# One encoder layer on one core: the early block's products in plain fp32 with its norm factor at the evacuations, late norms between the gates, and the ends of rows in pieces

## The chip, the cores and the metric

The kernel runs on one core of a Trainium2 chip. The core has a matrix engine (TensorE; PE in the rows, PEld for its weight loads), VectorE (DVE), ScalarE (ACT), GpSimd (POOL) and SyncE (SP), each with its own instruction stream, and 16 DMA engines that carry what the streams' queues ask for. The metric is the device time of one execution in microseconds; lower is better.

## The reference

One encoder layer over 512 tokens of 2048 channels, all in fp32:

```
h = rmsnorm(x, attn_norm)
q | k | v | z | gate = h @ w_in          # 1024 | 1024 | 1024 | 2048 | 4096 columns
A = diff_attention(q, k, v)              # 8 heads, two softmaxes each, block-causal
B = spatial_gating(gelu(z))              # u * (W_s @ rmsnorm(v) + b), chunks of 128 tokens
x = x + (sig(g_A) * (A @ P_A) + sig(g_B) * (B @ P_B)) @ w_out
x = x + peer(rmsnorm(x, ffn_norm))       # 8 heads, 16 of 16384 experts per token and head
y = rmsnorm(x, final_norm)
```

In `peer`, q = h @ w_q is scored against two sets of 128 sub-keys; the 16 best pairs give 16 experts per head and token, with a softmax over their scores as gates. Expert e adds gelu(h · u_e) * gate * v_e. The inputs are as the reference draws them, some of them scaled.

## The kernel before, in words

The first 128 tokens (the early block, names with E or 0) go through everything up to their experts first; the other 384 (the late block, L) follow. Weights come as tiles of 512 KB, `raw`, on SP's DMA queue. Each tile is split into two parts of the format fp32r: ACT casts it to `wh`, VectorE subtracts that from `raw` and gets `wl`, and each product is three matmuls: high weights by high operand, high by low, low by high (`project_rows` L174 for the early block, with the operand `hE` as two parts; `mm3` for the late one). `wh` and `wl` have three buffers, `raw` four and, in the early part, three more.

The order of the early block is: load x, norm it (Square with sum on ACT, rsqrt on VectorE with one POOL step, scale by the factor and by `gain`, a broadcast of attn_norm), transpose and split into `hE` (L494 to L503); queries, keys, values (`qk`, `ve`); two products `vv` with the attention heads between them and two `uu` (L559 to L568); then eight pairs of a `gate` and a `branch` product (L590 to L600). At the start of that stage the three late norms stand (L584 to L588): each loads 128 tokens `xt` on ACT's queue, norms them and fills a part of `hh`, which the late block multiplies by. Then `wo`, the second norm, four `wq` products with the top-k searches, and `route`, which lists experts and gates.

The late block: attention, `merge` (16 gate/branch pairs for each of two branches), output product, `wq`. Of the late tokens' experts 96 sets of single rows are taken for some tokens, and the others are done densely: all experts' u (products `pa`, 256 steps of 24 matmuls) and all experts' v (products `pvt`, 256 steps). During the u steps two generators hand out pieces of other work: `rgen` (the late tokens' routing; a step earns a credit and pieces cost some) and `ggen` (gates as dense columns, `gs`, written to `g_d`). The product of u, after Gelu, is written to `ga_d`; the v stage reads `ga_d` (`vga`) and `g_d` (`vg`, 1152 KB, one for each group of 16 steps).

The experts that are taken row by row ("sets") are fetched by POOL's indirect DMAs into `gat` tiles; each set costs VectorE one 128x2048 product (L267 with u, L274 with v). `sparse_step` is called once per weight load and takes as many sets as `due` says, which interpolates between `knots` (L247): pairs of a load's number and how many sets are done by then. 240 loads lie before the u steps (`AT_U`).

In the v stage the ends of rows stand at fixed steps. At step 26 the early block's experts (`acc0`, which is `h2n`) get x1 added and are normed and written (`finish_rows` L1025). When the last set of a group has been added, `fold_rows` (L1031) sums the partitions of `accx` by four matmuls with a 0/1 matrix, ACT copies them back, and `finish_rows` follows at once. `weights` casts and splits two steps ahead of the products.

## Time and profile before

| | |
|---|---|
| median of 3 runs | 3428.65 us (3427.03 to 3431.07) |
| the profiled execution | 3429.19 us, span 3427.5 us |
| TensorE matmul busy | 3250.8 us, 95% |
| VectorE busy | 2879.8 us, 84% |
| ScalarE, GpSimd busy | 1624.9 us (47%), 646.9 us (19%) |
| mean granted clock of TensorE | 0.977 |
| moved by DMA | 1099.54 MB, 321 GB/s over the span |

The span is the time between the first and last instruction seen by the profiler; the execution's own time is 1.7 us longer. Stages, by the output tiles of TensorE: x0 and its norm to 23.4 us; q, k, v to 100.9; vv and uu with the heads to 166.4; gate and branch to 336.3; wo to 385; wq and top-k 390.2 to 460.3; late attention to 719; merges to 1278; output product to 1410; late wq 1425 to 1582; u steps to 2535; v steps to 3411. A stretch is read by its rows of busy time: where TensorE's falls short of the stretch's length or its granted clock (1.00 is 2.4 GHz, 0.50 is 1.2 GHz) is below 1.00, it has lost time. The time in square brackets at the end of a row is how long the engine stood idle before it, and what ended that.

### The profile page before, as it was taken

The page shows a single profiled execution, that of the slowest core. Times are in us where ns is not written, and L with a number is a line of the kernel's source. Part 1 is how long each engine was busy: PE and PEld are TensorE (multiplying, and loading weights), DVE is VectorE, ACT ScalarE, POOL GpSimd, SP SyncE. Part 2 cuts the span into 40 slices and gives each one's busy share as a digit, 9 for nine tenths or more (in the row PEclk, how much of TensorE's full clock was granted, in tenths as well). Part 3 has the DMA queues.
Part 4 walks back from the last instruction along what each step waited for, and adds up shares of the span by engine and source line. Part 5 has one row for each costly group of instructions (what it writes and reads, how often), then busy time and mean ns, then how long its engine had stood idle before and what let it go on. Part 6 is the DMA issues. An engine that isn't in the chain of part 4 may idle for free. (4 is left out here: it accounts for less than half of the span.)

```text
span 3427.5 us, 53633 instructions
## 1 busy us (share of the span) xinstructions
PE 3250.8 (95%) x20673; PEld 3056.0 (89%) x20673; DVE 2879.8 (84%) x3851; ACT 1624.9 (47%) x2431; POOL 646.9 (19%) x507
## 2 busy tenths in 40 slices
PE   7979899989999999899899999999899999989997
PEld 5757678879989998799889999999898999989997
DVE  7878887888888889899899998777768899979974
ACT  6767634332233233333453788887343333333333
POOL 0000000222232223323223322222221111111100
PEclk9999999999999999899999999999999999999998
DMA  8779843869999999898899999999999999989953
GB/s 314 270 287 354 316 154 99 302 234 360 367 354 344 363 364 415 308 333 317 307 338 348 321 360 378 371 373 378 375 326 336 340 361 360 347 295 364 359 208 129
DMA packets 280784, 1099.54 MB, mean 321 GB/s; under 512 B 28144, under 2 KB 81392, under 8 KB 217744
## 3 DMA queue, kind: packets, MB, share of 16 engines
q1 hardware_dynamic: 189664, 560.14, 45.0%
q0 software_dynamic: 66656, 481.47, 37.1%
q10 hardware_dynamic: 24208, 54.50, 4.3%
q8 instruction: 163, 2.67, 0.3%
q14 instruction: 93, 0.76, 0.1%
HBM read 1048.98 MB, written 46.92 MB: 320 GB/s over the span
## 5 line engine op out<-in xcount | busy, mean ns | idle before, releaser
L109 DVE TENSOR_TENSOR wl<-raw,wh 128x1024 fp32r<-128x1024 f32 x992 | 1204.7, 1221 | 381.7 <-ACT wh L804 244.6
L804 ACT CAST wh<-raw 128x1024 fp32r<-128x1024 f32 x512 | 536.6, 1050 | 809.6 <-PE pvt L1051 329.1
L145 ACT CAST wh<-raw 128x1024 fp32r<-128x1024 f32 x480 | 502.0, 1050 | 686.7 <-PE gate L159 187.9
L160 PE MATMUL pa<-h2H,wl 128*128 128x288 f32 x2048 | 615.5, 301 | 27.0 <-DVE wl L109 26.7
L158 PE MATMUL pa<-h2H,wh 128*128 128x288 f32 x2048 | 616.5, 301 | 15.6 <-ACT wh L804 15.6
L1050 PE MATMUL pvt<-aH,wh 128*128 128x288 f32 x2048 | 612.9, 299 | 12.1 <-ACT wh L804 12.1
L1052 PE MATMUL pvt<-aH,wl 128*128 128x288 f32 x2048 | 607.5, 297 | 6.2 <-DVE wl L109 6.2
L159 PE MATMUL pa<-h2L,wh 128*128 128x288 f32 x2048 | 609.4, 298 | 0.0
L1051 PE MATMUL pvt<-aL,wh 128*128 128x288 f32 x2048 | 606.3, 296 | 0.0
L160 PEld LDWEIGHTS pa<-h2H,wl 128*128 128x128 f32 x2048 | 389.1, 190 | 37.1 <-DVE wl L109 35.5
L158 PEld LDWEIGHTS pa<-h2H,wh 128*128 128x128 f32 x2048 | 389.5, 190 | 16.8 <-ACT wh L804 16.8
L1050 PEld LDWEIGHTS pvt<-aH,wh 128*128 128x128 f32 x2048 | 389.3, 190 | 14.2 <-ACT wh L804 13.5
L1052 PEld LDWEIGHTS pvt<-aH,wl 128*128 128x128 f32 x2048 | 390.2, 191 | 8.7 <-DVE wl L109 8.6
L1051 PEld LDWEIGHTS pvt<-aL,wh 128*128 128x128 f32 x2048 | 390.7, 191 | 0.5 <-issue 0.5
L159 PEld LDWEIGHTS pa<-h2L,wh 128*128 128x128 f32 x2048 | 389.5, 190 | 0.0
L274 DVE SCALAR_TENSOR_TENSOR h2n<-gat,slot_a,h2n 128x2048 f32<-128x2048 f32 x127 | 297.7, 2344 | 5.2 <-DMA gat<-in_v_emb,slot_e 5.2
L288 POOL DMA_INDIRECT gat<-in_v_emb,slot_e x128 | 204.4, 1597 | 484.1 <-DVE wl L109 266.0
L267 DVE SCALAR_TENSOR_TENSOR gat<-gat,h2n 128x2048 f32<-128x2048 f32 x128 | 293.2, 2291 | 0.0
L288 POOL DMA_INDIRECT gat<-in_u_emb,slot_e x128 | 151.9, 1187 | 446.8 <-DVE gat L267 315.5
L288 POOL DMA_INDIRECT gat<-in_u_emb,xslot_e x96 | 146.4, 1525 | 437.1 <-DVE wl L109 423.6
L274 DVE SCALAR_TENSOR_TENSOR accx<-gat,xslot_a,accx 128x2048 f32<-128x2048 f32 x96 | 224.9, 2342 | 1.3 <-DMA gat<-in_v_emb,xslot_e 1.2
L267 DVE SCALAR_TENSOR_TENSOR gat<-gat,score 128x2048 f32<-128x2048 f32 x96 | 219.3, 2284 | 4.7 <-DMA gat<-in_u_emb,xslot_e 4.7
(423 smaller groups left out, 5889.6 us busy)
## 6 DMA issues: line engine op xcount, KB each, us to landing
raw<-in_uT SPq DMA_DIRECT2D x256, 512.0 KB, 8.0
raw<-in_v_tiles SPq DMA_DIRECT2D x256, 512.0 KB, 6.8
raw<-in_e_nat SPq DMA_DIRECT2D x144, 512.0 KB, 5.1
raw<-in_w_nat SPq DMA_DIRECT2D x128, 512.0 KB, 5.9
raw<-in_w_in SPq DMA_DIRECT2D x112, 512.0 KB, 6.9
ga_d<-ga ACTq DMA_DIRECT2D x128, 144.0 KB, 6.7
g_d<-gs ACTq DMA_DIRECT2D x18, 1024.0 KB, 10.1
vg<-g_d SPq DMA_DIRECT2D x16, 1152.0 KB, 13.8
```

The lines of the kernel that those rows point to most:

```text
L109: return nc.vector.tensor_tensor(low, full, high.bitcast(F32), op=OP.subtract)
L145: nc.scalar.copy(hi, raw)
L158: mm(ps, hi[:, k, :], xh[:, k0 + k, c0:c1], start=first and k == 0, stop=False)
L159: mm(ps, hi[:, k, :], xl[:, k0 + k, c0:c1], start=False, stop=False)
L160: got = mm(ps, lo[:, k, :], xh[:, k0 + k, c0:c1], start=False, stop=last and k == 7)
L267: used = nc.vector.scalar_tensor_tensor(row, row, 1.0, h2n if g < 0 else h2x[g], op0=OP.mult, op1=OP.mult, accum_out=a)
L274: used = nc.vector.scalar_tensor_tensor(acc, row, a, acc, op0=OP.mult, op1=OP.add)
L288: got = nc.gpsimd.indirect_dma_start(out=row, out_offset=None, in_=items[i][0], in_offset=bass.IndirectOffsetOnAxis(ap=column(i, slot_e, x ...
L804: nc.scalar.copy(hi, src)
L1050: mm(pv, hi[:, j, :], aH, start=j == 0, stop=False)
L1051: mm(pv, hi[:, j, :], aL, start=False, stop=False)
L1052: mm(pv, lo[:, j, :], aH, start=False, stop=j == VG - 1)
```

## The change

- The start: x comes in four pieces of 512 columns on SP's and ACT's queues. Each piece is transposed as it is, scaled by attn_norm as a column (`gcol`, 128x16, on POOL's queue) into `hP` and split into `hE`. The norm factor `r0` is worked out beside that and multiplied in where the products are evacuated (the `scale` of mul, Gelu and Sigmoid). The 1 MB broadcast is gone.
- `vv`, `uu` (two each) and the four `wq` products take `raw` and the plain fp32 operand (`hP`, `h2P`): one matmul instruction per k-tile, no `wh`, no `wl`.
- The late norms stand behind the gate/branch pairs (0,0), (0,3) and (1,2); `gainL` and `xt` are loaded on POOL's queue.
- `knots`: sets begin at load 14 instead of 24, and 212 instead of 204 are done at the first u step.
- `merge` computes a gate one pair ahead of its branch.
- `vg` is loaded on ACT's queue instead of SP's.
- `rgen` has three more pauses of cost 1.8, around the Exp of the softmax and ahead of the transposes, and a step earns 1.8 instead of 1.7.
- The ends of rows are generators, moved on by one piece a step.

```diff
-    def load_split_ap(src, shape):
+    def load_raw(src, shape):
...
         nc.sync.dma_start(raw, src)
+        return raw
+
+    def load_split_ap(src, shape):
+        raw = load_raw(src, shape)
...
     def row_product(src, xx, name):
         ps = pp_tile(name)
-        project_rows(src, xx, [ps])
+        if isinstance(xx, tuple):
+            project_rows(src, xx, [ps])
+            return ps
+        nk = 2 * src.shape[0]
+        for kk in range(nk // 2):
+            w = load_raw(src[kk], [P, 2, 512])
+            for j in range(2):
+                k = 2 * kk + j
+                mm(ps, xx[:, k, :], w[:, j, :], start=k == 0, stop=k == nk - 1)
         return ps
...
-    knots = [(24, 0), (AT_U, 204), (AT_V - 8, U_END), (AT_V, U_END), (AT_V + 222, len(items))]
+    knots = [(14, 0), (AT_U, 212), (AT_V - 8, U_END), (AT_V, U_END), (AT_V + 222, len(items))]
...
+        yield 1.8
         nc.scalar.activation(gate, gate, AF.Exp)
+        yield 1.8
...
-    nc.sync.dma_start(x0, x[0:P, :])
+    for q, eng in enumerate((nc.sync, nc.scalar, nc.sync, nc.scalar)):
+        eng.dma_start(x0[:, 512 * q:512 * q + 512], x[0:P, 512 * q:512 * q + 512])
...
+    hP = h2n.rearrange("p (k t) -> p k t", k=KT)
+    for q in range(KT // 4):
+        ks = slice(4 * q, 4 * q + 4)
+        pt = transpose4(x0[:, 512 * q:512 * q + 512])
+        nc.vector.tensor_tensor(hP[:, ks, :], pt, gcol[:, ks].unsqueeze(2).to_broadcast([P, 4, P]), op=OP.mult)
+        split_pair(hE, (slice(None), ks, slice(None)), hP[:, ks, :])
     with tc.tile_pool(name="e1", bufs=1) as e1:
-        gain = e1.tile([P, D], F32, name="gain")
-        nc.scalar.dma_start(gain, bcast_rows(attn_norm, D))
-        hn = e1.tile([P, D], F32, name="hn")
-        norm_columns(hn, x0, row_scale(hn, x0), gain, 0, hE)
+        sqx = e1.tile([P, D], BF16, name="sqx")
+        r0 = ea.tile([P, 1], F32, name="r0")
+        nc.vector.tensor_copy(r0, row_scale(sqx, x0))
...
-            nc.scalar.copy(nat, row_product(src, hE, "qk"))
+            nc.scalar.mul(nat, row_product(src, hE, "qk"), r0)
...
-            nc.scalar.activation(vv[:, cs], row_product(w_nat[Z_NAT + c], hE, "vv"), AF.Gelu)
+            nc.scalar.activation(vv[:, cs], row_product(w_nat[Z_NAT + c], hP, "vv"), AF.Gelu, scale=r0)
...
-        nc.scalar.dma_start(gainL, bcast_rows(attn_norm, D))
-        for b in range(LB):
-            xt = em.tile([P, D], F32, name="xt")
-            nc.scalar.dma_start(xt, x[(b + 1) * P:(b + 2) * P, :])
+        nc.gpsimd.dma_start(gainL, bcast_rows(attn_norm, D))
+        xts = []
+
+        def fetch(b):
+            xts.append(em.tile([P, D], F32, name="xt"))
+            nc.gpsimd.dma_start(xts[b], x[(b + 1) * P:(b + 2) * P, :])
+
+        def norm_late(b):
             hn = em.tile([P, D], F32, name="hnL")
-            norm_columns(hn, xt, row_scale(hn, xt), gainL, b, hh)
+            norm_columns(hn, xts[b], row_scale(hn, xts[b]), gainL, b, hh)
+            if b + 1 < LB:
+                fetch(b + 1)
+
+        fetch(0)
...
+                if (br, c) in ((0, 0), (0, 3), (1, 2)):
+                    norm_late((3 * br + c) // 2)
...
-        h2E = operand(e2p, KT, P, "h2E", ("eH", "eL"))
-        norm_columns(h2n, x0, rsqrt(ss, 1, 1.0 / D, "xr"), gain, 0, h2E)
+        h2P = e2p.tile([P, KT, P], F32, tag="eH", name="h2P")
+        r = rsqrt(ss, 1, 1.0 / D, "xr")
+        for q in range(KT // 4):
+            qs = slice(q * 512, (q + 1) * 512)
+            nc.vector.scalar_tensor_tensor(h2n[:, qs], x0[:, qs], r, gain[:, qs], op0=OP.mult, op1=OP.mult)
+            nc.scalar.copy(h2P[:, 4 * q:4 * q + 4, :], transpose4(h2n[:, qs]))
...
-            nc.scalar.copy(nat, row_product(e_nat[EW + c], h2E, "wq"))
+            nc.scalar.copy(nat, row_product(e_nat[EW + c], h2P, "wq"))
...
+            ahead = [unit(0)]
             for n in range(KT):
-                pg = project(w_in[G0 + KT * br + n], hh, "gate")
-                sg = gt.tile([P, LN], F32, name="sg")
-                nc.scalar.activation(sg, pg, AF.Sigmoid)
+                if n + 1 < KT:
+                    ahead.append(unit(n + 1))
+                sg = ahead[n]
...
-            nc.sync.dma_start(
+            nc.scalar.dma_start(
                 gms[grp], g_d[:, :, grp * VG:(grp + 1) * VG, :].rearrange("c p e t -> p c e t"))
...
-                credit += 0.0 if i < 2 else 1.7
+                credit += 0.0 if i < 2 else 1.8
...
-        def finish_rows(acc, t0, n):
+        def finish_rows(acc, t0, n, before):
+            for _ in before():
+                yield
             scr = gat.tile([P, D], F32, tag="gat", name="gat")
...
+            nc.scalar.activation(scr, acc, AF.Square, accum_out=ss)
+            yield
...
+            nc.gpsimd.tensor_tensor(y, v, mhalf, op=OP.pow)
+            yield
...
+            nc.vector.scalar_tensor_tensor(scr, acc, y, fgain, op0=OP.mult, op1=OP.mult)
+            yield
+            yield
             nc.scalar.dma_start(out[t0:t0 + n, :], scr[:n, :])
...
         def fold_rows(accx, fold):
+            yield
             for q in range(4):
...
                 nc.scalar.copy(accx[:, cs], ps)
+                if q % 2:
+                    yield
...
+                ends.append(finish_rows(acc0, 0, P, add_first))
+            ends[:] = [e for e in ends if next(e, "end") != "end"]
             sparse_step(AT_V + step, folded)
```

Three places show how instructions moved. The first is ACT's stream at the start of the gate stage, behind the last two evacuations of uu (`utE`); `hnL` is the Square of a late norm, `hH` the evacuated transposes of one, `sgE` a gate's Sigmoid. Before:

```order
L583 DMA gainL<-in_attn_norm 128x2048
L586 DMA xt<-in_x 128x2048
L145 CAST wh<-raw 128x1024 x2
L212 ACTIVATE hnL,ss<-xt 128x2048
L145 CAST wh<-raw 128x1024 x2
L203 CAST hH<-pt 128x4x128
L145 CAST wh<-raw 128x1024
L203 CAST hH<-pt 128x4x128 x2
L586 DMA xt<-in_x 128x2048
L203 CAST hH<-pt 128x4x128
```

The same place now:

```order
L151 CAST wh<-raw 128x1024 x6
L226 ACTIVATE hnL,ss<-xt 128x2048
L624 ACT_TABLE_LOAD
L624 ACTIVATE sgE<-gate,r_185 128x512
L151 CAST wh<-raw 128x1024 x2
L217 CAST hH<-pt 128x4x128 x2
L151 CAST wh<-raw 128x1024 x3
L217 CAST hH<-pt 128x4x128 x2
L226 ACTIVATE hnL,ss<-xt 128x2048
```

The loads have left ACT's stream, six casts stand between uu and the first Square, and the second Square follows the first norm's last evacuation directly.

The second place is the first load of `vg`, late in the u steps. Before, on SP, among the weight tiles:

```order
L794 DMA raw<-in_uT 128x1024 x221
L911 DMA vg<-g_d 128x18x128
L794 DMA raw<-in_uT 128x1024 x2
L906 DMA vga<-ga_d 128x576
L794 DMA raw<-in_uT 128x1024 x2
```

Now, on ACT, where `g_d<-gs` is the write of the last gates and `ga` a Gelu of u products:

```order
L847 CAST wh<-raw 128x1024
L909 DMA g_d<-gs 128x2048
L847 CAST wh<-raw 128x1024
L938 ACTIVATE ga<-pa 128x288
L939 DMA ga_d<-ga 128x288
L954 DMA vg<-g_d 128x18x128
L847 CAST wh<-raw 128x1024 x2
```

The load stands two weight casts behind the write of the gates that it reads, and ahead of the next casts.

The third is ACT's stream at the first fold in the v stage; `accx<-yps` copies the folded rows back, `gat,ss<-accx` is their Square. Before:

```order
L804 CAST wh<-raw 128x1024 x3
L1036 COPY accx_24162<-yps 128x512 x4
L212 ACTIVATE gat,ss<-accx_24162 128x2048
L1029 DMA out_y<-gat 64x2048
L804 CAST wh<-raw 128x1024
```

Now:

```order
L847 CAST wh<-raw 128x1024
L1104 COPY accx_23650<-yps 128x512 x2
L847 CAST wh<-raw 128x1024
L1104 COPY accx_23650<-yps 128x512 x2
L847 CAST wh<-raw 128x1024
L1073 ACTIVATE gat,ss<-accx_23650 128x2048
L847 CAST wh<-raw 128x1024
L969 CAST aH<-vga 128x288 x2
L847 CAST wh<-raw 128x1024 x3
L954 DMA vg<-g_d 128x18x128
L1088 DMA out_y<-gat 64x2048
```

A cast of weights now stands between each two pieces, and the write of the rows is four casts behind the Square.

## Rows read from the trace of the kernel before

**Rows 1.** The page: busy time by engine, DMA share by slice, one group.

```profile
PE 3250.8 (95%) x20673; PEld 3056.0 (89%) x20673; DVE 2879.8 (84%) x3851; ACT 1624.9 (47%) x2431; POOL 646.9 (19%) x507
...
DMA  8779843869999999898899999999999999989953
...
L109 DVE TENSOR_TENSOR wl<-raw,wh 128x1024 fp32r<-128x1024 f32 x992 | 1204.7, 1221 | 381.7 <-ACT wh L804 244.6
```

**Rows 2.** Stretches: length, busy PE, PEld, DVE, ACT, POOL, PEclk, DMA share, GB/s.

```profile
100.90:166.40 65.50, 59.22 (x251) 44.26 (x251) 55.42 (x95) 47.83 (x74) 3.48 (x3) 0.92 0.75 250
166.40:336.30 169.90, 150.09 (x646) 115.81 (x645) 140.49 (x151) 119.54 (x128) 1.65 (x3) 0.96 0.88 321
230.90:336.30 105.40, 104.09 (x446) 81.57 (x445) 93.04 (x84) 79.42 (x81) 0.00 (x0) 1.00 0.98 356
390.20:460.30 70.10, 60.13 (x245) 47.60 (x246) 62.27 (x198) 37.51 (x41) 0.00 (x0) 0.86 0.62 216
1690.00:2090.00 400.00, 377.54 (x2755) 369.93 (x2754) 382.61 (x677) 262.59 (x473) 112.49 (x68) 0.98 0.93 342
2090.00:2400.00 310.00, 310.00 (x2377) 310.00 (x2377) 238.38 (x226) 254.47 (x474) 70.81 (x51) 1.00 0.98 376
2400.00:2535.00 135.00, 125.01 (x905) 122.92 (x904) 98.12 (x98) 48.07 (x66) 29.08 (x21) 0.97 0.96 364
2535.00:2690.00 155.00, 143.08 (x1036) 140.82 (x1035) 115.90 (x136) 60.26 (x87) 26.57 (x20) 0.96 0.91 324
...
3036.00:3066.00 30.00, 21.40 (x103) 16.69 (x102) 17.99 (x25) 9.68 (x13) 2.92 (x4) 0.83 0.48 148
3290.00:3312.00 22.00, 17.27 (x83) 13.54 (x83) 11.53 (x17) 8.09 (x11) 0.56 (x1) 0.82 0.29 88
```

**Rows 3.** Timeline of the start: start, us, engine, line, instruction, idle before.

```profile
11.75 1.91 ACT L212 ACTIVATE hn<-x 128x2048 f32<-128x2048 f32 x1 [9.21 <-DMA x<-in_x]
...
23.40 0.80 PE L183 MATMUL qk<-wh,hEH 128*128 128x512 f32 x1
```

**Rows 4.** Timeline: first passes of two k-tiles of a split product, full clock.

```profile
28.23 0.39 PE L183 MATMUL qk<-wh,hEH 128*128 128x512 f32 x1
...
28.93 0.40 PE L183 MATMUL qk<-wh,hEH 128*128 128x512 f32 x1
```

**Rows 5.** Timeline: weight loads of a plain fp32 product (second fold), full clock.

```profile
3297.30 0.19 PEld L1035 LDWEIGHTS yps<-accx,fold 128*128 128x128 f32 x1 [0.36 <-issue]
3297.73 0.19 PEld L1035 LDWEIGHTS yps<-accx,fold 128*128 128x128 f32 x1 [0.24 <-issue]
```

**Rows 6.** Timeline of wq: the first of three such waits.

```profile
416.65 0.79 PE L184 MATMUL wq<-wl,h2EH 128*128 128x512 f32 x1 [3.31 <-DVE wl L109]
```

**Rows 7.** Timeline of the gate stage: transposes of the first late norm.

```profile
188.04 1.09 PE L196 MATMUL pt<-ident,hnL 128*128 128x128 f32 x4 [11.07 <-DVE hnL L222]
```

**Rows 8.** Timeline at the end of the late attention.

```profile
753.72 0.87 PE L196 MATMUL pt<-ident,o 128*128 128x128 f32 x3 [5.79 <-DVE o L481]
```

**Rows 9.** Groups of 1581.8 to 2535; waits of 1655 to 2090 (total, times, longest).

```profile
L274 DVE SCALAR_TENSOR_TENSOR h2n<-gat,slot_a,h2n 128x2048 f32<-128x2048 f32 x56 | 131.3, 2345 | 3.5 <-DMA gat<-in_v_emb,slot_e 3.5
...
PEld pa L160 <- DVE wl L109: 31.5, 34, 3.0
```

**Rows 10.** DMA issues (KB, median us to landing), vg's of 2385 to 2415; timeline.

```profile
raw<-in_uT SPq DMA_DIRECT2D x256, 512.0 KB, 8.0
...
g_d<-gs ACTq DMA_DIRECT2D x18, 1024.0 KB, 10.1
...
vg<-g_d SPq DMA_DIRECT2D x1, 1152.0 KB, 20.7
...
2414.11 0.61 PE L158 MATMUL pa<-h2H,wh 128*128 128x288 f32 x1 [5.82 <-ACT wh L804]
```

**Rows 11.** Timeline of the v stage: behind acc0's end, and the first fold.

```profile
2639.22 0.61 PE L1050 MATMUL pvt<-aH,wh 128*128 128x288 f32 x1 [6.28 <-ACT wh L804]
...
3045.22 6.74 PE L1035 MATMUL yps<-accx,fold 128*128 128x512 f32 x8 [5.44 <-DVE accx L274]
```

More of the change, by code (lines that the diff above doesn't have):

```diff
@@ L69, in hybrid_block @@
     nc.gpsimd.dma_start(subln, diff_subln)
+    gcol = const.tile([P, KT], F32, name="gcol")
+    nc.gpsimd.dma_start(gcol, attn_col)
     gmn = const.tile([P, GROUPS], F32, name="gmn")
@@ L418, in route @@
                     nc.scalar.dma_start(xslot_g[g][to, :], gf[of])
+        yield 1.8
         pt = pt_tile("prt")
@@ L1023, in final_gain, with add_first @@
                 nc.vector.tensor_mul(ys[b][:c1 - c0, cs], ys[b][:c1 - c0, cs], fgain[:c1 - c0, cs])
-        def finish_rows(acc, t0, n):
+        def finish_rows(acc, t0, n, before):
+            for _ in before():
+                yield
             scr = gat.tile([P, D], F32, tag="gat", name="gat")
-            r = row_scale(scr, acc)
-            nc.vector.scalar_tensor_tensor(scr, acc, r, fgain, op0=OP.mult, op1=OP.mult)
-            nc.scalar.dma_start(out[t0:t0 + n, :], scr[:n, :])
+            ss = small.tile([P, 1], F32, name="ss")
+            nc.scalar.activation(scr, acc, AF.Square, accum_out=ss)
+            yield
+            v = small.tile([P, 1], F32, name="nrv")
+            y = small.tile([P, 1], F32, name="nry")
+            t = small.tile([P, 1], F32, name="nrt")
+            nc.vector.tensor_scalar(v, ss, 1.0 / D, EPS, op0=OP.mult, op1=OP.add)
+            nc.gpsimd.tensor_tensor(y, v, mhalf, op=OP.pow)
+            yield
+            nc.vector.tensor_mul(t, y, y)
+            nc.vector.tensor_mul(t, t, v)
+            nc.vector.tensor_scalar(t, t, -0.5, 1.5, op0=OP.mult, op1=OP.add)
+            nc.vector.tensor_mul(y, y, t)
+            nc.vector.scalar_tensor_tensor(scr, acc, y, fgain, op0=OP.mult, op1=OP.mult)
+            yield
+            yield
+            nc.scalar.dma_start(out[t0:t0 + n, :], scr[:n, :])
+        def add_first():
+            first = gat.tile([P, D], F32, tag="gat", name="gat")
+            nc.scalar.dma_start(first, x1_d[:P, :])
+            for _ in range(5):
+                yield
+            nc.vector.tensor_add(acc0, acc0, first)
+            yield
         def fold_rows(accx, fold):
+            yield
             for q in range(4):
@@ L1036, in fold_rows @@
                 nc.scalar.copy(accx[:, cs], ps)
+                if q % 2:
+                    yield
+        ends = []
         def folded(g):
-            fold_rows(accx[g], folds[g])
-            finish_rows(accx[g], *XG[g])
+            ends.append(finish_rows(accx[g], *XG[g], lambda: fold_rows(accx[g], folds[g])))
         for step in range(KT * NG):
@@ L1073, in hybrid_block @@
             if step == 20:
-                first = gat.tile([P, D], F32, tag="gat", name="gat")
-                nc.scalar.dma_start(first, x1_d[:P, :])
-            if step == 26:
-                nc.vector.tensor_add(acc0, acc0, first)
-                finish_rows(acc0, 0, P)
+                ends.append(finish_rows(acc0, 0, P, add_first))
+            ends[:] = [e for e in ends if next(e, "end") != "end"]
             sparse_step(AT_V + step, folded)
@@ L1083, in hybrid_block @@
                     nc.scalar.dma_start(ys[b][:c1 - c0, :], x1_d[T0 + c0:T0 + c1, :])
-        assert eaten[0] == len(items), (eaten, len(items))
+        assert eaten[0] == len(items) and not ends, (eaten, len(items))
         settle(*before)
```

15 lines of the change are left out of this document (10 added, 5 removed).

## The prediction, on record before the changed kernel ran

> **What bounds the kernel now.** I read the page's totals first, then the stretches with their granted clock, then the rows where TensorE stands still. The totals say that TensorE is the bound on the whole: 95% busy, VectorE 84%, and the DMA engines at 8 to 9 tenths in most slices [rows 1]. So the kernel's time is TensorE's work at full clock plus what it loses, and the loss of a stretch has two parts that the row of a stretch gives: length less busy time (idle), and (1 − PEclk) × length (a granted clock below 2.4 GHz; the records go between 1.00 and 0.50, 2.4 and 1.2 GHz). From [rows 2], idle + clock in us: vv and uu of the early block (100.9–166.4) 6.3 + 5.2; gate/branch with the late norms (166.4–336.3) 19.8 + 6.8; wq (390.2–460.3) 10.0 + 9.8; the middle of the u products (1690–2090) 22.5 + 8.0; their end (2400–2535) 10.0 + 4.0; the first v products (2535–2690) 11.9 + 6.2; the two folds (3036–3066, 3290–3312) 8.6 + 5.1 and 4.7 + 4.0. That is 131 us in places that the edits touch. In 2090–2400 TensorE has no gap and the DMA share is 0.98: a place where nothing is to be had.
>
> **The change part by part.** Durations are of the profiled execution: span 3427.5 and 1.7 around it, 3429.19, which is 0.5 over the median of the three runs. A minus is time gained.
>
> Start. The first product starts at 23.40, 9.7 us after the Square's end (11.75 + 1.91) [rows 3]. The Square has waited for x, 1 MB that lands together with the 1 MB gain, which is gone. The transposes and the column scaling now need no Square, but in VectorE's order the norm's small steps, the fold sums and two wl (1.22 each, [rows 1]) stand ahead of the first scaled piece, and the first of them waits for the Square. Without the gain I take the landing 3 us earlier, and 5 of the 9.7 us off: −8. Bounds −3 (only the landing) and −11 (8 of the 9.7 as well).
>
> Plain products (two vv, two uu, four wq). A split product is three passes per k-tile; starts 28.23 and 28.93 are one k-tile apart, 0.70 [rows 4], so 16 × 0.70 = 11.2 us. A plain fp32 product shows two weight loads and passes per 512 columns, 0.43 apart at full clock [rows 5]: 16 × 2 × 0.43 = 13.8. Each plain product so costs TensorE 2.6 more: +10.3 for four. What it takes away: 16 casts (1.05) and 16 wl (1.22) per two products. For vv and uu that is 32 × 1.22 = 39 us of VectorE in a stretch of 65.5 where it was busy 55.4 [rows 2]; the idle + clock of 11.5 is what can come back. +10.3 against 10: I take 0, bounds −6 (more of the stretch's weight waits vanish) and +10 (nothing comes back). For wq the loss is 19.8, with three waits of 3.31 us for a wl that stands behind the top-k searches [rows 6]; a plain product needs no wl at all, so the searches no longer stand ahead of the weights. +10.3 − 18.3 = −8, bounds +2 and −12.
>
> Late norms. They go from a block of three at the start of the gate stage to one behind each of three pairs, and their loads to POOL's queue, the gain ahead of uu. Now TensorE waits 11.07 us for the first one's transposes [rows 7], since ACT's queue waits for xt with the casts behind it. Six undisturbed pairs take 105.4, 17.57 a pair [rows 2]: eight take 140.5. The 48 transposes at half the 1.09 of four [rows 7] (it ran at the lower clock) add 48 × 0.14 = 6.5: 147. The DMA floor: 169.9 us × 321 GB/s are 54.5 MB, at the 356 GB/s of the undisturbed pairs 153 us. VectorE's 140.5 fits in. So 147 to 153 instead of 169.9, I take 152: −18. In the new order a Square stands right behind its predecessor's last evacuation on ACT, so it may wait for an xt that was just asked for: bounds −6 (two such waits of some 5 us, half of the stage's loss) and −23 (147).
>
> Merge. The last head's chain costs a gap of 5.79 [rows 8]; one more gate product now stands ahead of the first branch, and the sets on VectorE come at other places. −2, bounds −6 and +6.
>
> u stage. 212 instead of 204 sets lie ahead of it: 8 × 2.345 = 18.8 us of VectorE [rows 9] go from the u products into attention and merge, and the route's steps have three more pauses. TensorE waits there for wl, 34 times and 31.5 us between 1655 and 2090 [rows 9], where VectorE is busy 382.6 of 400. Half of the sets' time and a little for the pauses: −12. Bounds −25 (nearly all of that wait) and +8 (the sets sit on the merge's weights instead, and DMA holds the stage).
>
> vg on ACT's queue. The first vg (1152 KB) took 20.7 us on SP's queue and TensorE stood 5.82 us for the raw tile behind it [rows 10]; with the lower clock after it the loss is near 9. On ACT's queue the raw tiles have SP's to themselves: −7. Against it: in ACT's order it stands ahead of casts, one step behind the write of g_d that it has to wait for, and such a write lands after 10.1 us [rows 10]; the splits are two steps ahead, 6.4 us (2377 matmuls, 24 a step, in 310 us [rows 2] are 3.13 a step, 3.2 with the gaps). So up to 4 for one hold: bounds −12 (the second vg's small waits as well) and +4. The Trainium skill (DMA: Bandwidth & Descriptors, "Issuing engines are not separate DMA queues") says that all issues share the same 16 engines and another issuing engine saves only issue time. The trace has raw tiles landing after 8.0 us by the median and 20.7 for the vg, and does not say whether the wait is order in one queue or bandwidth. By that rule the term is 0 and the sum 7 us less.
>
> v stage. The first rows' end (acc0) put a Square, five small steps and a 128x2048 product in one place: TensorE stood 6.28 us [rows 11] and ran at the lower clock for some time after; −8 of the stretch's 18.1. Each fold waits for its last accumulation (5.44 the first, [rows 11]), runs four plain products in a row at the lower clock, and ACT's evacuation, Square and output stand ahead of the next cast. In pieces of two products, one piece a step, the accumulation has a step to end, and the casts go between: 22.4 us of loss [rows 2], I take −17 of it. Bounds for both −30 and −12.
>
> Sum: −8 + 0 − 8 − 18 − 2 − 12 − 7 − 25 = −80; 3429.2 − 80 = 3349.
>
> **The rivals.** *DMA takes its part.* The late stages run at 0.93 to 0.98 of the DMA engines [rows 2], and what TensorE gains there the loads don't give: u and vg fall away (+19), the late norms bring −8 (+10), the start −5 (+3): −48, 3381. For it: those shares. Against: slices with gaps are those where the share falls.
> *More comes back.* VectorE was what held the early block, and each wl gone counts: vv/uu −6, late norms −23, wq −12, u −20: −103, 3326. For it: VectorE's 62 of 70 us in wq; against: each needs its bound at once.
> *The early block pays.* The plain passes stand as they are and the waits turn into others (top-k searches are still VectorE's): vv/uu +10, wq +2: −60, 3369.
> *Slower: plain products at the lower clock.* Place: the eight plain products. In the first fold eight passes took 6.74, 0.84 each [rows 11], all at 1.2 GHz. Were TensorE granted only that through vv, uu and wq, each takes 32 × 0.84 = 26.9 instead of 11.2: 8 × 15.7 = +125, less the idle 16.3 that goes: +109, with the other terms (−72) +37: 3466. It decides from a mean clock of 0.62 over these products on (8 × 13.8 / c − 8 × 11.2 − 16.3 = 72). For it: wq has a clock of 0.86 today. Against: the clock falls in this trace behind gaps, and the plain products take gaps away.
>
> **How the numbers follow.** The forecast 0.53, DMA 0.22, more back 0.12, early block pays 0.09, lower clock 0.04. The forecast's own spread is about 20 to either side; down to 3320 takes in half of the case 3326 and up to 3392 the case 3381 with its spread, so some 14% are left out. What a measurement of this kernel can tell from no change is 0.2%, 6.9 us. The slower case holds 0.04; from the tails of the DMA and early cases 0.02 are within 0.2%; faster 0.94.
>
> **What would show it.** Right: first product near 15.5; the stretch of vv and uu still near 65 with fewer weight waits; gate/branch near 152; wq without 3.31 waits and near 62; fewer waits for wl in the middle of u; no gap behind the first vg; no TensorE gap over 2 us at the three ends in v; the page's clock above 0.977. Wrong: ACT waiting for xt or for g_d's landing with casts behind it; the plain products at 0.5; idle time of TensorE that comes back in 1700–2400 as waits for raw tiles.

## The result, and the profile after

The changed kernel takes 3373.75 us (median of 4 runs, 3371.23 to 3376.36) against 3427.84 (4 runs): a ratio of 0.9842, interval 0.9825 to 0.9859. It is 54 us faster where 80 were predicted; the profiled execution (3376.36, span 3374.7) gains 52.8 of span. The mean granted clock went from 0.977 to 0.987.

The table sets the stages side by side, each from its first TensorE instruction to the next one's (us); the merges end with the output product's last matmul.

| stage | before | after | change | predicted |
|---|---|---|---|---|
| to the first product | 23.4 | 15.4 | −8.0 | −8 |
| q, k, v | 77.4 | 80.3 | +2.9 | 0 |
| vv, uu | 65.8 | 64.6 | −1.2 | 0 |
| gate/branch with late norms | 169.6 | 156.5 | −13.1 | −18 |
| wo and second norm | 55.8 | 56.1 | +0.3 | 0 |
| wq | 68.1 | 59.7 | −8.4 | −8 |
| late attention | 259.2 | 261.7 | +2.5 | −2 |
| merges to output product | 691.3 | 702.9 | +11.6 | (in that −2) |
| late wq | 171.1 | 172.9 | +1.8 | 0 |
| u steps | 953.0 | 947.9 | −5.1 | −19 (u −12, vg −7) |
| v steps | 876.3 | 840.1 | −36.2 | −25 |
| end | 16.5 | 16.6 | +0.1 | 0 |

The page's busy line after, which answers to the first of [rows 1]: TensorE has 5 us less to do and VectorE 77 us.

```profile
PE 3245.8 (96%) x20545; PEld 3012.0 (89%) x20545; DVE 2803.2 (83%) x3784; ACT 1561.5 (46%) x2367; POOL 681.0 (20%) x512
```

Stretches of after, with the columns of [rows 2]:

```profile
15.40:95.70 80.30, 76.68 (x336) 59.37 (x334) 68.96 (x92) 55.66 (x74) 1.14 (x1) 1.00 0.90 321
95.70:160.20 64.50, 62.87 (x188) 29.32 (x187) 24.94 (x65) 19.10 (x41) 3.16 (x4) 1.00 0.80 272
160.20:316.80 156.60, 148.74 (x644) 115.46 (x644) 138.34 (x149) 118.08 (x127) 3.38 (x6) 0.98 0.94 342
372.40:432.80 60.40, 60.40 (x169) 28.47 (x167) 25.97 (x164) 6.66 (x10) 0.00 (x0) 0.98 0.74 246
694.30:1397.20 702.90, 691.85 (x3668) 650.56 (x3667) 596.02 (x565) 223.40 (x290) 208.13 (x160) 0.99 0.93 351
1690.00:2390.00 700.00, 677.41 (x5123) 666.02 (x5123) 606.66 (x912) 516.64 (x945) 184.28 (x113) 1.00 0.95 350
2390.00:2518.00 128.00, 116.19 (x825) 114.20 (x825) 89.57 (x90) 43.26 (x59) 33.95 (x17) 0.95 0.97 362
2518.00:2690.00 172.00, 167.90 (x1249) 166.67 (x1248) 141.45 (x167) 70.88 (x99) 35.43 (x25) 0.99 0.95 348
3014.00:3044.00 30.00, 30.00 (x211) 28.08 (x210) 24.88 (x33) 11.75 (x15) 7.62 (x5) 1.00 0.90 322
```

Against [rows 2]: the stretch of vv and uu has the same length, but TensorE is now busy in 62.9 of 64.5 us where it was busy in 59.2 of 65.5, with VectorE down from 55.4 to 24.9. The stretch of wq has no gap left and its clock is 0.98 instead of 0.86. The place of the first fold (3014 to 3044) has no gap at all. Two stretches are at odds with the prediction: 2390 to 2518 still loses 11.8 us of TensorE and 0.05 of the clock, and the merges, where the shares hardly differ, are longer by 11.6.

The same stretch of merges before, for comparison:

```profile
719.30:1410.60 691.30, 681.41 (x3656) 642.08 (x3655) 597.65 (x570) 222.49 (x288) 202.78 (x159) 0.99 0.95 357
```

TensorE's idle time is 9.9 us before and 11.1 after: of the 11.6 us, only one is a wait. The rest is busy time, 10.4 us more for the same products (x3668 and x3656 are the records that the trace kept).

The late gates and uu products are the plainest to compare: 384 matmuls in a row, all at full clock. A row of one tile gives the duration of one (least/median/most, ns) and the first and last start. Before, and then after:

```profile
L158 PE MATMUL uu<-hH,wh x128: 333/334/422, 1004.4 to 1076.4; 128*128 128x384 f32 x128
```

```profile
L164 PE MATMUL uu<-hH,wh x128: 335/338/423, 985.4 to 1058.5; 128*128 128x384 f32 x128
```

72.0 us for 381 intervals in the one, 73.1 in the other. From start to start, the mean over a stage without its slowest and fastest tenth, that is 173.4 against 176.4 ns here, 173.3 against 176.7 in the gates of the merges, 226.7 against 228.9 in the output products, and the other way round in the u steps: 133.4 against 132.3. The instructions and the granted clock are the same. What differs is where buffers lie: `gcol`, 64 bytes a partition, stands in the pool of constants, ahead of the weight buffers, and moves them by 64 bytes; the late operand `hh` is allocated from the other end and doesn't move.

At the end of the u steps ACT's rows answer to [rows 10]. ACT waits for the landing of `g_d`, issues `vg`, and then its next issue, a small write, holds the queue for 7.83 us:

```profile
2402.16 0.38 ACTq L954 DMA_DIRECT2D vg<-g_d  x1
2402.66 2.08 ACT L847 CAST wh<-raw 128x1024 fp32r<-128x1024 f32 x2 [7.71 <-DMA g_d<-gs]
...
2405.07 7.83 ACTq L939 DMA_DIRECT2D ga_d<-ga  x1
2413.30 1.99 ACT L847 CAST wh<-raw 128x1024 fp32r<-128x1024 f32 x2 [8.26 <-PE pa L166]
...
2446.85 6.12 ACTq L939 DMA_DIRECT2D ga_d<-ga  x1
...
2466.19 1.04 ACT L847 CAST wh<-raw 128x1024 fp32r<-128x1024 f32 x1 [10.15 <-DMA vg<-g_d]
```

The casts that TensorE needs stand behind each of these: gaps of 3.05, 1.50 and 4.61 us follow, where [rows 10] had one of 5.82.

At the start, three rows show VectorE's order: the Square ends at 9.8, the first scaled piece (VectorE) runs at 13.85 behind the norm's steps and two splits, and at 24.52 TensorE has waited for the third tile's `wl`, which stands behind the pieces and their splits.

```profile
7.86 1.91 ACT L226 ACTIVATE sqx<-x 128x2048 bf16<-128x2048 f32 x1
...
13.85 0.69 DVE L521 TENSOR_TENSOR h2n<-pt,gcol 128x512 f32<-128x512 f32 x1
...
24.52 0.50 PE L190 MATMUL qk<-wl,hEH 128*128 128x512 f32 x1 [3.62 <-DVE wl L111]
```

### The profile page after: what moved, and what is told of

The parts are those of the page before. It is cut to its first block, busy times and chain, and to the rows that moved or that the text cites. A ratio compares the mean times of both kernels' runs of the same rounds, so it can differ in the third digit from the quotient of the medians.

```text
span 3374.7 us, 53163 instructions
## 1 busy us (share of the span) xinstructions
PE 3245.8 (96%) x20545; PEld 3012.0 (89%) x20545; DVE 2803.2 (83%) x3784; ACT 1561.5 (46%) x2367; POOL 681.0 (20%) x512
## 5 line engine op out<-in xcount | busy, mean ns | idle before, releaser
L111 DVE TENSOR_TENSOR wl<-raw,wh 128x1024 fp32r<-128x1024 f32 x928 | 1128.2, 1222 | 399.8 <-ACT wh L847 234.5
L847 ACT CAST wh<-raw 128x1024 fp32r<-128x1024 f32 x512 | 536.8, 1049 | 811.3 <-PE pvt L1122 301.4
L151 ACT CAST wh<-raw 128x1024 fp32r<-128x1024 f32 x416 | 435.0, 1050 | 679.6 <-PE gate L165 183.5
L166 PE MATMUL pa<-h2H,wl 128*128 128x288 f32 x2048 | 613.8, 300 | 25.4 <-DVE wl L111 24.9
L302 POOL DMA_INDIRECT gat<-in_u_emb,slot_e x128 | 164.2, 1283 | 590.5 <-DVE gat L281 267.9
L302 POOL DMA_INDIRECT gat<-in_u_emb,xslot_e x96 | 162.7, 1695 | 463.3 <-DVE wl L111 455.8
L302 POOL DMA_INDIRECT gat<-in_v_emb,xslot_e x96 | 105.0, 1094 | 598.3 <-DVE wl L111 590.3
```

The costliest lines, as they stand in the source:

```text
L111: return nc.vector.tensor_tensor(low, full, high.bitcast(F32), op=OP.subtract)
L151: nc.scalar.copy(hi, raw)
L166: got = mm(ps, lo[:, k, :], xh[:, k0 + k, c0:c1], start=False, stop=last and k == 7)
L302: got = nc.gpsimd.indirect_dma_start(out=row, out_offset=None, in_=items[i][0], in_offset=bass.IndirectOffsetOnAxis(ap=column(i, slot_e, x ...
L847: nc.scalar.copy(hi, src)
```

## The experiments

Ratios are to the kernel before on the same chip; the changed kernel's is 0.9842 (0.9825 to 0.9859). Seventeen runs of the kernel before on one chip range from 3419 to 3437 us, and the runs were on several chips, so small effects are read from stages. A stage varies too, in kernels whose edits don't touch it: the u steps take 940.5 to 949.6 us in six profiles with the changed kernel's u steps, the v steps 835.3 to 843.2 in six with its v steps, gate/branch 153.5 to 157.6. Each stage below is one profile; a difference inside such a spread is not shown by it.

**The place of the weight buffers.** `e1_pad256` gives `gcol` 256 bytes, so that the weight buffers are back at the old place modulo 256 bytes.

```diff
-    gcol = const.tile([P, KT], F32, name="gcol")
+    gcol = const.tile([P, 64], F32, name="gcol")[:, :KT]
```

> The changed kernel with the new constant gcol given 256 bytes a partition instead of 64, nothing else. That puts the weight buffers wh and wl back at the same place modulo 256 bytes, relative to the late operand, as in the kernel before. Theory A (place): the 64 bytes are why a matmul of the merges takes 176.7 ns in the changed kernel and 173.3 before, and one of the u steps 132.3 instead of 133.4. Expected: 173 and 133.4 again; attention's end to the late wq (702.9 us) some 9 shorter, u steps some 6 longer, total near 3371. Rival B (order or traffic: the sets earlier, the gate ahead of its branch): the spacing stays at 176.7 and the time at 3374, within 2.

Measured: 3367.95 (0.9828, 0.9811 to 0.9845), an interval that overlaps the changed kernel's; the stages tell them apart. The same row of uu:

```profile
L164 PE MATMUL uu<-hH,wh x128: 331/334/423, 981.0 to 1053.1; 128*128 128x384 f32 x128
```

Gates 173.4, uu 173.4, output product 226.7, u steps 133.4 ns: the numbers of the kernel before, within 0.1. Merges to output product take 695.0 us instead of 702.9, where four other kernels with the changed order and 64 bytes take 701.1 to 702.5. Theory A holds for the spacing; that the u steps would get some 6 us longer is not seen (943.5, inside their spread).

`e12_before64` is the reverse: the kernel before and 64 unused bytes.

```diff
+    spare = const.tile([P, KT], F32, name="spare")
+    nc.gpsimd.memset(spare, 0.0)
```

> The kernel before, with 64 unused bytes a partition (set once by GpSimd) where the changed kernel has gcol, and nothing else of the change: every later buffer stands 64 bytes further. Theory A (place alone sets the spacing): the late gates go from 173.3 to about 176.7 ns a matmul, u steps from 133.3 to 132.3; merges to late wq some 10 us longer (691.3 before), u steps some 5 shorter, total 3430 to 3436. Rival B (it takes the changed order as well): 173.3 and 133.3 as before, total as before within 3.

Measured: 3435.90 (1.0024, 1.0012 to 1.0036): slower than before, by 64 bytes that nothing reads.

```profile
L160 PE MATMUL uu<-hH,wh x128: 334/338/424, 1006.8 to 1079.8; 128*128 128x384 f32 x128
```

Gates 175.9, uu 176.3, u steps 132.4 ns; merges to output product 697.2 (before 691.3). Rival B has fallen: no other edit is needed.

`e9_pad128` and `e10_pad192` (both on `e8_mix` below, `gcol` at 128 and 192 bytes) ask for the rule.

```diff
-    gcol = const.tile([P, 64], F32, name="gcol")[:, :KT]
+    gcol = const.tile([P, 32], F32, name="gcol")[:, :KT]      # e10_pad192: 48
```

> e8_mix with gcol at 128 bytes instead of 256: the weight buffers stand 128 bytes (modulo 256) from the late operand hh in the merges and at the same place as the operand's slice in the u steps (which begins 384 bytes into a row of hh). Theory A (the distance modulo 256 decides, as the branch products suggest, which take 175.7 at a distance of 128 in all runs): gates 175.7 ns, u steps below 132.3; merges, products and late wq some 7 us longer than in e8_mix, u steps some 7 shorter or more. Theory B (only the distance modulo 128 counts): gates 173.3, u steps 133.3, no difference from e8_mix (3348). Rival C (place has nothing to do with it): any other numbers.

> e8_mix with gcol at 192 bytes: distance 192 (modulo 256) in the merges, 64 in the u steps. Theory A: gates neither 173.3 nor 175.7 (64 gave 176.7), u steps not 133.3 (128) nor what e9_pad128 shows. Theory B (distance modulo 128: same as 64): gates 176.7, u steps 132.3 as in the changed kernel, total 3345 to 3355. Rival C: as for e9_pad128.

Measured: 3362.12 (0.9807, 0.9787 to 0.9826) and 3356.34 (0.9797, 0.9783 to 0.9812). Mean spacing in ns by bytes that the weight buffers are moved:

| moved by | gates | output product | u steps |
|---|---|---|---|
| 0 (before), 256 | 173.3 | 226.7 | 133.4 |
| 64 (eight profiles) | 175.9 to 176.7 | 228.9 | 132.3 |
| 128 | 175.7 | 231.9 | 131.7 |
| 192 | 173.3 | 233.3 | 133.4 |

Theory A had the gates right at 128 and failed at 192 (173.3, where it excluded that); theory B failed at 128. Place matters, with a period that 256 bytes complete, and differently for each pair of operand and weights; the rule behind it stays open. No place is best for all stages. Of the totals, `e8_mix` with 256 bytes is below both; but `e11_start` below, also with 256 and on the same chip as these two, has 0.9764 to 0.9793, which overlaps the interval of 192, so the best place is not shown.

**vg's queue.** `e2_vg_sp` puts the loads back on SP.

```diff
-            nc.scalar.dma_start(
+            nc.sync.dma_start(
                 gms[grp], ...
```

> The changed kernel with the vg loads back on SP's queue. Theory A (the queue's own stream pays): on ACT the vg issue waits 7.7 us for the write of g_d, the ga_d issue behind it takes 7.8 us, and casts stand behind both; TensorE loses 18 us between 2390 and 2518. On SP the loss should be that of before, some 14: 4 us less, total near 3370. Rival B (bandwidth: the 1152 KB cost the same from any queue): no change, 3374 within 2. Rival C (the prediction): SP's order is worse, 7 us more, 3381.

Measured: 3383.39 (0.9875, 0.9858 to 0.9893), 9.6 us longer by the medians. The two stages part: the u steps gain 9.4 us (938.5), the v steps lose 18.5 (858.6). The second is far outside the spread of the v steps (835.3 to 843.2). The first is not: 938.5 lies only 2.0 below the lowest other profile, and of the 9.4 us 6.7 fall in the last 48 steps, where the vg loads are (table under the knots). Theory A has the direction right for the u steps, with an open size; the prediction is right for the v steps, B for neither. ACT's hold is plain all the same: in all seven profiles with the first two vg on ACT's queue, two of the 128 writes `ga_d<-ga` take 2.8 to 10.2 us to issue; in the seven with them on SP's, none takes more than 0.37. In v, waits for `wl` come back with vg on SP; waits of 2535 to 3360 in this kernel and then in the changed one (total, times, longest):

```profile
ACT wh L847 <- DMA raw<-in_v_tiles: 130.5, 57, 10.8
...
PEld pvt L1123 <- DVE wl L111: 15.4, 14, 1.8
```

```profile
ACT wh L847 <- DMA raw<-in_v_tiles: 109.2, 47, 7.7
...
PEld pvt L1123 <- DVE wl L111: 4.1, 4, 2.6
```

On ACT's queue a vg takes longer to land, 25.0 us by the median of 2540 to 3330 against 13.1 before. The weight tiles land after 7.0 us before and 7.1 in the changed kernel by the median of all; but those issued within 8 us behind a vg took 11.6 before (20 tiles) and 8.7 in the changed kernel (30). The long load is stretched, and the tiles pass it.

**The ends of rows.** `e3_ends` has `finish_rows`, `fold_rows` and acc0's end as before.

```diff
-                ends.append(finish_rows(acc0, 0, P, add_first))
-            ends[:] = [e for e in ends if next(e, "end") != "end"]
+                first = gat.tile([P, D], F32, tag="gat", name="gat")
+                nc.scalar.dma_start(first, x1_d[:P, :])
+            if step == 26:
+                nc.vector.tensor_add(acc0, acc0, first)
+                finish_rows(acc0, 0, P)
...
         def folded(g):
-            ends.append(finish_rows(accx[g], *XG[g], lambda: fold_rows(accx[g], folds[g])))
+            fold_rows(accx[g], folds[g])
+            finish_rows(accx[g], *XG[g])
```

> The changed kernel with the ends of rows as before: acc0's end in one place at step 26, folds and row ends in one piece. The v stage took 876.3 us before, 840.1 in the changed kernel and 858.6 with vg on SP, so vg's queue alone is worth 18.5 of the 36.2 there. Theory A (the two add up): the ends in pieces are worth the other 18, and the v stage takes some 858 here, total near 3390. Rival B (the prediction, ends alone 25): 865, total 3399. Rival C (vg's queue made the gaps at the folds harmless too): under 845, total under 3380.

Measured: 3396.46 (0.9901, 0.9886 to 0.9916), v steps 860.3: theory A. Both gaps are back:

```profile
2615.03 0.61 PE L1093 MATMUL pvt<-aH,wh 128*128 128x288 f32 x1 [5.26 <-ACT wh L847]
...
3015.85 6.70 PE L1078 MATMUL yps<-accx,fold 128*128 128x512 f32 x8 [3.47 <-DVE accx L288]
```

But they don't cost the same. The v steps by groups of 16, from one group's last accumulation to the next one's, the first from the start of v (us; the 16th group, 63.2 before and 61.4 after, is left out):

| groups | before | after | e3_ends | e2_vg_sp |
|---|---|---|---|---|
| 1 to 4 (acc0's end in the 2nd) | 226.0 | 213.4 | 214.6 | 221.5 |
| 5 to 9 | 253.5 | 254.8 | 256.0 | 257.4 |
| 10, 11 (first fold) | 118.6 | 104.6 | 115.3 | 109.3 |
| 12 to 14 | 151.9 | 152.4 | 152.5 | 152.5 |
| 15 (second fold) | 63.3 | 53.4 | 60.5 | 53.4 |

The folds in one piece cost 10.7 and 7.1, some 18 (16 to 18 against the six profiles with the ends in pieces). acc0's end in one place costs 1.2 of the first four groups against the changed kernel, although its gap is 5.26; against the six profiles (207.7 to 214.9) it is anything up to 7. That the loads set the pace there (0.95 of the DMA engines in 2518 to 2690) would explain a small cost, but no run tests it. The larger part of what the first groups gained came from vg's queue (8.1 of 12.6).

**The plain products.** `e4_split` has vv, uu and wq on `hE` and `h2E` again.

```diff
-row_product(w_nat[Z_NAT + c], hP, "vv")
+row_product(w_nat[Z_NAT + c], hE, "vv")
...
-row_product(e_nat[EW + c], h2P, "wq")
+row_product(e_nat[EW + c], h2E, "wq")
```

> The changed kernel with vv, uu and wq as split products again (hE, h2E). The prediction: vv and uu the same either way, wq 8 us longer, total 3382. Theory A (from the traces: the plain products leave no idle time, 62.9 of 64.5 and 60.4 of 60.4 us busy, at nearly full clock): vv and uu 65 to 66 as before, wq 68; total 3382 to 3384. Rival B: with the other edits the split products run undisturbed and need their 11.2 us each: vv and uu near 58, wq near 60, total 3368.

Measured: 3384.07 (0.9856, 0.9838 to 0.9874). Stretches of vv/uu and wq, with the columns of [rows 2]:

```profile
97.60:163.20 65.60, 59.61 (x254) 44.66 (x253) 55.80 (x96) 48.25 (x74) 4.08 (x4) 0.92 0.77 271
376.70:445.10 68.40, 58.48 (x237) 45.92 (x237) 60.20 (x196) 36.86 (x40) 0.00 (x0) 0.87 0.62 209
```

And from its timeline the first of wq's waits, which answers to [rows 6]:

```profile
401.47 0.79 PE L190 MATMUL wq<-wl,h2EH 128*128 128x512 f32 x1 [3.30 <-DVE wl L111]
```

1.0 us for vv and uu and 8.8 for wq, with the idle time and the clock of before: theory A and the prediction in the stages. (The intervals of the two totals overlap.)

**The late norms.** `e5_norms` puts them back in a block, with their loads on ACT's queue (the old loop of three instead of `norm_late` behind three pairs).

```diff
-        nc.gpsimd.dma_start(gainL, bcast_rows(attn_norm, D))
...
+        nc.scalar.dma_start(gainL, bcast_rows(attn_norm, D))
+        for b in range(LB):
+            xt = em.tile([P, D], F32, name="xt")
+            nc.scalar.dma_start(xt, x[(b + 1) * P:(b + 2) * P, :])
             hn = em.tile([P, D], F32, name="hnL")
...
+            norm_columns(hn, xt, row_scale(hn, xt), gainL, b, hh)
...
-                if (br, c) in ((0, 0), (0, 3), (1, 2)):
-                    norm_late((3 * br + c) // 2)
```

> The changed kernel with the three late norms in a block at the start of the gate stage again, loads on ACT's queue. The stage took 169.6 us before and 156.5 in the changed kernel. Theory A (their place is the whole gain): near 169, total 3386. Rival B (part of it comes from elsewhere, such as a gain and uu's weights no longer in its way): 160 to 164, total 3378 to 3381.

Measured: 3383.74 (0.9869, 0.9851 to 0.9886), the stage 170.2 us: theory A. The gap of [rows 7] is back:

```profile
182.09 1.09 PE L210 MATMUL pt<-ident,hnL 128*128 128x128 f32 x4 [10.27 <-DVE hnL L236]
```

**The knots and the merges' order.** `e6_knots` and `e7_merge` undo one each.

```diff
-    knots = [(14, 0), (AT_U, 212), ...
+    knots = [(24, 0), (AT_U, 204), ...
```

> The changed kernel with the knots as before: sets begin at load 24, 204 done at the first u step. The prediction: 8 sets more among the u products cost there some 9 to 12 us, total near 3385. Theory A (read from the two traces: the u steps' idle time is the same, 22.6 against 22.5 us in 1690 to 2390, though 8 sets fewer lie there): nothing is lost in u, and the late attention gets back its 2 us; total 3372 to 3376.

Measured: 3374.74 (0.9857, 0.9838 to 0.9875): no difference in the total that can be told. The u steps take 949.9 instead of 947.9. By steps, counted by the Gelus of their products (one for two steps), in us:

| u steps | before | after | e6_knots | e2_vg_sp | five other kernels with after's u steps |
|---|---|---|---|---|---|
| 1 to 128 | 494.5 | 482.6 | 491.1 | 482.4 | 480.7 to 484.8 |
| 129 to 208 | 291.4 | 294.4 | 289.6 | 291.9 | 290.5 to 296.1 |
| 209 to 256 (vg) | 167.1 | 170.9 | 169.2 | 164.2 | 165.8 to 172.2 |

The first 128 steps before, after, and in this kernel, with the columns of [rows 2]:

```profile
1581.70:2076.20 494.50, 461.94 (x3355) 452.58 (x3354) 467.22 (x786) 290.85 (x503) 143.22 (x82) 0.97 0.91 334
```

```profile
1570.10:2052.70 482.60, 450.30 (x3321) 437.97 (x3321) 446.54 (x767) 274.86 (x463) 141.30 (x78) 0.99 0.91 330
```

```profile
1566.30:2057.40 491.10, 453.62 (x3327) 442.04 (x3326) 456.66 (x767) 274.87 (x464) 140.62 (x82) 0.98 0.91 334
```

In these steps the change brought 11.9 us, and the old knots lose 8.5 of them, with 10.1 us more work for VectorE. The idle time is the same before and after (32.6 and 32.3); what fell is TensorE's busy time, at a granted clock of 0.99 instead of 0.97. So the reading of theory A, equal idle time in 1690 to 2390, left out the clock, and a stretch of fixed time does not hold the same steps in both kernels. Some of the gain is work that moved: 34 matmuls fewer are recorded here, and steps 129 to 208, where TensorE has hardly a gap in either kernel, take 3.0 us more. With the old knots these steps get 4.8 back and the merges 4 (220.8 us for the first 16 pairs instead of 225.2): the knots gain in u what they cost elsewhere. No run undoes the pauses of `rgen` and its credit, so the 3.4 us of the 11.9 that stay with the old knots have no shown cause; place alone does not bring them (498.1 in `e12_before64`).

```diff
-            def unit(n):
+            for n in range(KT):
+                pg = project(w_in[G0 + KT * br + n], hh, "gate")
                 sg = gt.tile([P, LN], F32, name="sg")
...
-            ahead = [unit(0)]
-            for n in range(KT):
-                if n + 1 < KT:
-                    ahead.append(unit(n + 1))
-                sg = ahead[n]
+                nc.scalar.activation(sg, pg, AF.Sigmoid)
```

> The changed kernel with merge in the old order (gate, then its branch, no gate ahead). The prediction: 2 us longer, 3376. Theory A: the order costs 2 to 3 us at the end of the attention, where two gates and a longer chain of waits stand (24.0 us for two gates), so 3371, and the merges' matmuls stay at 176.7 ns. Rival B: the order is what makes them 176.7: they go to 173, and the total to 3366.

Measured: 3372.81 (0.9849, 0.9831 to 0.9867), gates at 176.0 ns, the first 16 pairs 221.1 us: theory A in the stage (4 us shorter; to the output product's end it is 2.9 to 4.7 us below the changed kernel and the four others named under `e1_pad256`), no difference in the total.

**A version that beats both.** `e8_mix` takes `e1_pad256`, the first two vg loads on SP and the others on ACT, and a pause after each pair of the twelve small writes of the route. In the changed kernel these stand in one block on ACT, and the cast behind them starts after ACT has computed nothing for 16.82 us:

```profile
1677.33 1.04 ACT L847 CAST wh<-raw 128x1024 fp32r<-128x1024 f32 x1 [16.82 <-DMA xslot_g<-gate]
```

```diff
-            nc.scalar.dma_start(
+            (nc.sync if grp < 2 else nc.scalar).dma_start(
                 gms[grp], ...
...
                     nc.scalar.dma_start(xslot_g[g][to, :], gf[of])
+                    yield 0.9
```

> A version meant to beat both: the changed kernel with gcol at 256 bytes (weights at the old place modulo 256), the first two vg loads on SP's queue and the others on ACT's, and the 12 small xslot writes of the route handed out in pairs with a pause after each instead of in one block on ACT. From the runs: place -6, u steps of vg on SP -9, and the gap of 9.7 us before the cast behind the xslot writes with the lower clock after it, some -10. Sum: 3350. Rivals: the first vg loads on SP hold up v (nothing of the -9), 3358; the pairs on ACT still wait for ei, 3360.

Measured: 3348.42 (0.9753, 0.974 to 0.9766), the interval below the changed kernel's: u steps 930.7, v steps 836.2. Where TensorE had stood 9.73 us behind that block, its stretch is now nearly full, and the first 48 u steps take 167.6 us instead of 183.5:

```profile
1570.00:1690.00 120.00, 119.25 (x880) 117.28 (x880) 110.07 (x103) 47.50 (x61) 44.88 (x20) 1.00 0.94 343
```

Of the first vg loads a gap of 3.95 us is left at 2463, behind a cast that waits 9.59 for its tile to land. The last 48 steps take 168.0 us, inside the range of the kernels with vg on ACT's queue (165.8 to 172.2): the gain of the u steps comes mainly from the small writes, and moving the first two loads shows none of its own here.

`e11_start` is `e8_mix` with an order edge: the Square of x0 behind the last cast of its operand (for that, the two helpers around it are written out).

```diff
...
+        tc.add_manual_dep(sq.ins, got.ins.name, queued, reason="behind the operand")
...
```

> e8_mix with the Square of x0 put behind the last cast of its operand (an order edge on ACT, no other change). In the changed kernel x has landed at 6.4 us, but VectorE's first step waits for the Square until 9.7, and the scaling of the first piece runs at 13.7. Theory A (VectorE's queue behind the norm step is what the start waits for): first product near 11.5 instead of 15.2, q, k, v not longer, total 3344 to 3346. Rival B (the column gcol or the first weights' splits end last): first product at 14 or later, total as e8_mix, 3348. Rival C: the norm factor comes too late for the first evacuation, q, k, v longer by as much.

Measured: 3350.29 (0.9778, 0.9764 to 0.9793): no gain in the total. First product at 14.7 instead of 15.2, so rival B: VectorE's first step is now the first tile's split, which waits for that tile.

```profile
9.83 1.23 DVE L111 TENSOR_TENSOR wl<-raw,wh 128x1024 fp32r<-128x1024 f32 x1 [9.83 <-ACT wh L151]
...
13.23 0.68 DVE L522 TENSOR_TENSOR h2n<-pt,gcol 128x512 f32<-128x512 f32 x1
```

q, k and v take 79.0 us instead of 82.1, and TensorE's longest wait in them is 2.15 us instead of 4.07; the total does not show it.

## Why the prediction came out as it did

The direction and the range (3320 to 3392) were right, the size 26 us too large: a gain of 54 for 80. The time is nearer to the rival "DMA takes its part" (3381) than to the forecast (3349), but not for its reasons: it let the v stage stay at −25 and took u and vg as nothing. That the sum came out inside the range is in part luck, since two terms lay outside their own bounds in opposite directions (merge at +15.9; the v steps at −36.2, which holds what vg's queue gave there). By its own steps:

- *What is lost* (131): the losses listed there add up to 143; the forecast does not use the sum.
- *Start* (−8): the first product came 8.0 earlier, as said, but q, k, v took 2.9 us more. The step took an earlier start for a gain of all that follows. x landed at 6.4 us instead of 11.7, 5 us earlier and not 3, and the first weight tile at 8.9 instead of 12.8; but the third split of the weights, behind the operand's splits and the norm's steps on VectorE, began only 5.4 earlier (22.7 instead of 28.1), and TensorE, 8 us ahead by then, waited for it. The 3.62 us gap shows it, and in `e11_start` that gap moves and shrinks.
- *Plain products* (0 and −8): −1.2 and −8.4, and 1.0 and 8.8 when undone. The price of 0.43 us a pass and the loss that comes back were both right.
- *Late norms* (−18): −13.1, and 13.7 when undone. Mechanism right, a quarter too large: 7.9 us of idle time and 0.02 of the clock remained in the stage.
- *Merge* (−2): this step failed worst, attention to late wq came out at +15.9. Its own subject, the order, costs some 4 us in the first merges (`e7_merge`) instead of giving 2, and the earlier sets cost about as much (`e6_knots`), as the upper bound of the u step had named. The larger part no step had: 64 bytes of a new constant move the weight buffers, and each matmul of the late gates takes 2% longer. `e1_pad256` and `e12_before64` show that in both directions, 7.9 and 5.9 us in the stretch from the merges to the output product. The late attention's 2.5 us have no shown cause.
- *u steps* (−12): the first 128 steps, where the waits of [rows 9] are, brought 11.9, so the size was right there. The form was not: the idle time stayed, and the clock rose from 0.97 to 0.99. `e6_knots` takes 8.5 of it away, near the half of the sets' time that the step had put in (9.4). Of the rest of the stage's balance, steps 129 to 208 cost 3.0, and the last 48 cost 3.8 instead of giving vg's 7.
- *vg's queue* (−7): about −9 in all by `e2_vg_sp`, but by other places: the u steps lose (9.4 against one profile, at least 2 against the others), and the v steps gain 18.5. The prediction had seen ACT's hold and named it as a sign of being wrong, and priced it at up to +4; but ACT stood four times, 7.71 us for g_d, 7.83 and 6.12 in the issue behind each vg, and 10.15 that the profile puts down to the second vg's landing. Its bound of 6.4 us took all 2377 matmuls of the stretch for u products; 312 of them are others, so two steps are 7.2 us. That the later loads of vg hold up weight tiles in v was not in it: the loss of 2535 to 2690 in [rows 2] was there to be seen, and the prediction put 8 us of it down to acc0's end. The rule it weighed from the Trainium skill (DMA: Bandwidth & Descriptors, "Issuing engines are not separate DMA queues") would have made the queue worth only issue time; here the measurement decides against that reading, 18.5 us in one stage. Another section of the same page of the Trainium skill ("Queues, rings and completion order") says that each queue row has its own ring on each DMA engine and that a DMA engine takes from the rows in turn, and the landings above agree: vg went from 13.1 to 25.0 us, the tiles right behind it from 11.6 to 8.7.
- *v stage* (−25, acc0 −8 and folds −17): the folds brought 18, acc0's end 1.2 against one profile and at most 7 against the others. The other 17 of the 36.2 are about what vg's queue gave there (18.5 by `e2_vg_sp`).

So 18 of the missing us lie in the merge term, most of them in parts that no step had; some 7 at acc0's end, 5 in the late norms, and 3 each in q, k, v and the later u steps. vg's queue covered a part of this by something else that no step had, the weight tiles in v.

## What to carry to other kernels

Compare the same steps of work in two profiles, not the same stretch of time, and count the granted clock beside the idle time: the first 128 u steps gained 11.9 us with no change in idle time. A gap is not a price: the folds gave back some 18 of their 22.4 us of loss, but taking away a gap of 5 to 6 us at acc0's end gave between nothing and 7. A long load belongs on a queue of its own when nothing urgent stands behind it on the issuing engine (18.5 us in v); where casts stand behind it, as in u, the hold has to be counted against that. One profile for each kernel leaves several us of a long stage open, so a second profile of unchanged code is worth having before a small difference is explained. And when a stage that an edit doesn't touch changes by 1 or 2% at the same clock, compare the spacing of one matmul in both traces before explaining it by order: a new constant may have moved the buffers.

## What was not expected of the hardware

- Spacing of matmuls by the place of their buffers: 173.3 to 176.7 ns for 384 columns, 226.7 to 233.3 for 512, 131.7 to 133.4 for 288, at the same granted clock, when the weight buffers move by 64, 128 or 192 bytes; 256 restores it.
- An issue of a small DMA can hold its engine: 7.83 and 6.12 us on ACT's queue, 3 and 6 us behind a vg load, where the same issue takes 0.33 us elsewhere; two such issues in each of the seven profiles with the first vg loads on ACT, none in the seven without.
